# When a hybrid decoder step fetches the gate tiles of its attention projection, and when the rows of the projection after it

## The chip, the cores and the metric

The kernel runs on one core of a Trainium2 chip, as one launch. The metric is the device time of that launch in microseconds (us). Five engines work side by side and meet at semaphores: PE multiplies matrices (PEld is its weight load), DVE and ACT work elementwise, POOL works elementwise and issues accumulating transfers, SP only issues transfers. Each engine takes its instructions in the order in which they stand in its queue; an instruction whose data is late holds all that stand behind it.

## The reference, cut to what matters

One layer of a hybrid decoder on 512 prompt tokens and 8 x 4 sample tokens, 544 columns in all, in float32:

```
u   = x @ w_in                                   # queries, keys, values, gates of both branches
br_m = layernorm(mlstm(u)) * sigmoid(o_m) * silu(z_m)      # (544, 2048)
br_a = sliding_window_attention(u) * silu(z_a)             # (544, 2048)
y    = sigmoid(g_m) * (br_m @ w_proj_m) + sigmoid(g_a) * (br_a @ w_proj_a)
out  = layernorm(alpha * x + y @ w_out)
```

The change lies in `sigmoid(g_a) * (br_a @ w_proj_a)`, called the attention projection below, and at its border with `br_m @ w_proj_m`, the next projection. Both weights are 2048 x 2048. The kernel keeps float32 accuracy on a PE that multiplies a reduced format: each operand is split into a high part (`h`) and a low part (`l`), and a product is high x high + low x high + high x low.

## The kernel before, in words

Everything is stored transposed: an output tile is 128 of the 2048 output columns by 544 tokens, so a projection has 16 output tiles (`ct`). In the attention projection tiles 0 to 7 and 14, 15 are computed one by one (`plain_a`, 96 matmuls each), and tiles 8 to 13 two by two (`paired` over `pair_a`).

A pair computes its two tiles by seven half-size products instead of eight (Winograd's form of Strassen's scheme). The 2 x 2 blocks of the weights are `b11`, `b12`, `b21`, `b22` (128 x 8 x 128 each, 512 KB): two are loaded into buffers of the pool `wr` (tag `raw`, 3 of them), two into `wr2` (tag `raw2`, 3 of them), which also holds a sum, `t1`. `prepare` makes the weight sums, some on DVE (line 679), some by a transfer from POOL that adds in place (line 677, for `b12` += `b22` and `b21` += `b11`), and `split` casts a block to its high part on ACT (line 208, `wh`) and takes the low part on DVE (line 209, `wl`). `half_product` runs 16 matmuls with `wh` (line 699) and 8 with `wl` (line 701). `gather` collects banks into the two outputs `O1`, `O2`. When product 6 is done, `end` multiplies them by the gate tiles `sg` (line 1787, DVE) and stores the result to `d_t` (line 1788, SP). Product p of the first of the three pairs is called P0 to P6 here, and the pairs are the first, second and third.

The gate tiles are the stored `sigmoid(g_a)`, 128 x 544 each (272 KB), fetched by `early` (line 1782) into the pool `c5`, which has two buffers. A third gate tile therefore has to wait until the product of an earlier one has left for `d_t`. `paired` calls `early` at step 2 of a pair, or at the step that the pair names in `early_at`.

The activations of a pair are sums of the rows of `br_a` that were stored earlier (`stored_sums`, read back from `d_sa` by POOL, line 1732, and split on ACT and DVE, lines 257 and 258).

Around the pairs, two more streams of rows are fetched. `branch` (line 1463) loads the sixteen 272 KB rows of `br_m`, `d_brm`, for the next projection and splits them; `operand_sums` (line 1698) loads the same rows two at a time (544 KB) from POOL for the sums of that projection's pairs, two loads ahead.

The order of instructions within each queue is set by a scheduler, which places an instruction by its own timeline; `tc.issue_after(x)` keeps an instruction behind `x`, and `tc.high_priority` lifts it. `state["load"]` is the last weight load so far, `state["cast"]` and `state["split"]` the last weight split. So where the source calls a load need not be where it is issued: a load whose buffer is free can be issued far ahead of its place in the program.

Of the kernel before, what the change touches and what calls it, by code (L numbers as in the profile page):

```python
# [18 lines left out]
ALU = mybir.AluOpType  # L19
# [55 lines left out]
def _build(tc, nc, i, o, es):  # L75
# [12 lines left out]
    V, A, G, PE = nc.vector, nc.scalar, nc.gpsimd, nc.tensor  # L88
# [43 lines left out]
    state = {}  # L132

    def tick():

        with ExitStack() as place:
            if state.get("end"):
                place.enter_context(tc.issue_after(state["end"].ins))
            for g in list(live):
                if next(g, StopIteration) is StopIteration:  # L140
                    live.remove(g)

    def drain():
        while live:
            tick()
# [189 lines left out]
    for g in range(8):  # L335
        for q in range(2):
            k = g * 2 + q
# [321 lines left out]
    def raw2():  # L659
        return wr2.tile([128, 8, 128], F32, tag="raw2", name=nm("raw2"))  # L660

    def load_a(w):
        w["b11"], w["b12"] = (load_half(w["wv"], c0, 0) for c0 in (w["cA"], w["cB"]))

    def load_b(w):
        for n, c0 in (("b22", w["cB"]), ("b21", w["cA"])):
            w[n] = raw2()
            state["load"] = nc.sync.dma_start(w[n][:], w["wv"][:, 8:16, c0:c0 + 128])

    def prepare(w, n):  # L670


        def add(out, a, b):
            if w.get("acc") and out == a and n != 2:
                loaded = state.get(("sums", 13))
                with tc.issue_after(loaded.ins) if loaded else ExitStack():
                    G.dma_start(out=w[out][:], in_=w[b][:], accum_op=ALU.add)  # L677
            else:
                V.tensor_tensor(out=w[out][:], in0=w[a][:], in1=w[b][:], op=ALU.add)  # L679
        if n == 1:  # L680
            w["t1"] = raw2()
            add("t1", "b11", "b12")
        elif n == 2:
            add("b11", "t1", "b22")
        w["hl", n] = split(w[("b11", "t1", "b11", "b21", "b12", "b22", "b21")[n]])
        if n == (1 if w.get("acc") else 3):
            add("b12", "b12", "b22")
        elif n == (3 if w.get("acc") else 4):
            add("b21", "b21", "b11")
# [42 lines left out]
    def paired(work, plain=None, rest=()):  # L732

        steps = [(w, n) for w in work for n in range(7)]
        ready = 0
        with tc.issue_after(state["load"].ins):
            load_a(work[0])
            load_b(work[0])
        for at, (w, n) in enumerate(steps):

            while ready < min(at + 3, len(steps)):
                with tc.high_priority(offset=AHEAD), tc.issue_after(plain.ins) if plain else ExitStack():
                    prepare(*steps[ready])
                ready += 1
            p = at // 7 + 1
            if p < len(work):
                if n == 3:
                    load_a(work[p])
                elif n == 4:
                    load_b(work[p])  # L750
            if n == w.get("early_at", 2) and "early" in w:
# [602 lines left out]
    esF, ahead, PF = ExitStack(), [], KT  # L1354
# [97 lines left out]
    def branch(src, p, tmp, ahead=(), order=(0, 1, 2, 3)):  # L1452
        hs, los = [None] * 4, [None] * 4
        for q in order:
            hs[q], los[q] = (p.tile([128, 4, T], F32R, tag="act", name=nm(n)) for n in ("bh", "bl"))

        def steps():
            for k in range(KT):
                if k < len(ahead):
                    st = ahead[k]  # L1460
                else:
                    st = tmp(k)
                    nc.sync.dma_start(st[:], src[k])
# [205 lines left out]
    wm, wa_, wo = kview("w_proj_m"), kview("w_proj_a"), kview("w_out")  # L1669
# [21 lines left out]
    def operand_sums(src, to, p, far=2, pinned=False):  # L1691

        def behind(name):
            return tc.issue_after(state[name].ins) if pinned else ExitStack()

        def load(k):
            t_ = tx.tile([128, 2, T], F32, tag="tx", name=nm("tx"))
            G.dma_start(out=t_[:], in_=src[k:k + 9:8].rearrange("k p t -> p k t"))
            return t_

        ahead = [load(k) for k in range(far)]
        for k in range(8):
            for _ in range(2):
                yield
            t_ = ahead.pop(0)
            r11, r21, r12, r22 = (t_[:, a, c:c + HT] for a in range(2) for c in (0, HT))
            for name in ("s1", "n2", "n3", "s4"):
                if name not in to:
                    to[name] = quad(p, name)
            with behind("split"), behind("cast"):  # L1710
                four_sums(r11, r12, r21, r22, r22, r12)
                for name, r_ in (("s1", r22), ("n2", r11), ("n3", r21), ("s4", r12)):
                    hilo(r_, to[name][0][:, k], to[name][1][:, k])
            if k + far < 8:
                ahead.append(load(k + far))
# [58 lines left out]
    def pair_a(ct):  # L1774

        sgs = []

        def early():
            for c in (ct, ct + 1):
                sg = c5t()  # L1780
                with tc.issue_after(state["load"].ins):
                    nc.sync.dma_start(sg[:], d_sga[c])
                sgs.append(sg)

        def end(o1, o2):
            for c, sg, o in zip((ct, ct + 1), sgs, (o1, o2)):
                V.tensor_tensor(out=sg[:], in0=o[:], in1=sg[:], op=ALU.mult)
                nc.sync.dma_start(d_t[c], sg[:])
        return dict(wv=wa_, x=XA, cA=ct * 128, cB=ct * 128 + 128, scale=1.0, acc=True, end=end, early=early,
                    early_at=4)  # L1790

    LEAD_A, PAIR_A, TAIL_A = 6, 8, 14
    marks = []
# [39 lines left out]
    state["end"] = None  # L1833
    drain()
    esB2.close()
    tx = pool(esR, "txc", 2)
# [274 lines left out]
    for g in range(G3):  # L2111
        ct = 16 - G3 + g
# [125 lines left out]
```

## Time and profile before

| what | value |
|---|---|
| median of 3 runs | 2449.86 us (2449.78 to 2451.84) |
| the profiled execution | 2449.24 us, of which the span of instructions is 2447.5 us |
| PE busy | 2427.9 us, 99% of the span |
| DVE, ACT, POOL busy | 1910.0, 1252.3 and 532.5 us |
| granted TensorE clock, mean | 0.997 of full speed |
| transfers | 479.88 MB, mean 196 GB/s |
| three pairs of the attention projection | about 1971 to 2042 us of the span |

Times inside the span are counted in us from its start. A row of the timeline gives start, duration, engine, line, operation, output and inputs, and, in brackets, how long the engine had been idle and what released it. Matmuls overlap, so the distance from one start to the next is their pace, not the duration in the row. A row of the table of stretches gives the length of the stretch, the busy time of PE, PEld, DVE, ACT and POOL with the number of instructions, the granted clock, the busy share of the 16 DMA engines and the GB/s moved; the share can read a little over 1.

### The profile page before, as it was taken

The page shows a single profiled execution, that of the slowest core. Times are in us where ns is not written, and L with a number is a line of the kernel's source. Part 1 is how long each engine was busy: PE and PEld are TensorE (multiplying, and loading weights), DVE is VectorE, ACT ScalarE, POOL GpSimd, SP SyncE. Part 2 cuts the span into 40 slices and gives each one's busy share as a digit, 9 for nine tenths or more (in the row PEclk, how much of TensorE's full clock was granted, in tenths as well). Part 3 has the DMA queues.
Part 4 walks back from the last instruction along what each step waited for, and adds up shares of the span by engine and source line. Part 5 has one row for each costly group of instructions (what it writes and reads, how often), then busy time and mean ns, then how long its engine had stood idle before and what let it go on. Part 6 is the DMA issues. An engine that isn't in the chain of part 4 may idle for free.

```text
span 2447.5 us, 49023 instructions
## 1 busy us (share of the span) xinstructions
PE 2427.9 (99%) x19394; PEld 2374.8 (97%) x19394; DVE 1910.0 (78%) x2879; ACT 1252.3 (51%) x2074; POOL 532.5 (22%) x509
## 2 busy tenths in 40 slices
PE   8999999999999999999999999999999999999998
PEld 8999999999999999999999999999999999999997
DVE  7868888888888888987877888878766566877666
ACT  5456676676666665443433444544644444434432
POOL 3114334333333430211111221211000120111111
PEclk9999999999999999999999999999999999999999
DMA  6876666667777655677677586686765488898776
GB/s 178 202 173 158 160 163 148 160 152 177 169 171 177 165 145 144 153 228 241 180 251 242 167 244 208 187 248 213 249 203 168 168 244 244 233 235 271 200 218 204
DMA packets 569597, 479.88 MB, mean 196 GB/s; under 512 B 48664, under 2 KB 464136, under 8 KB 569112
## 3 DMA queue, kind: packets, MB, share of 16 engines
q1 hardware_dynamic: 550776, 411.22, 56.8%
q0 software_dynamic: 18112, 64.76, 13.5%
q8 instruction: 152, 2.49, 0.4%
q10 hardware_dynamic: 480, 0.79, 0.1%
q14 instruction: 77, 0.63, 0.1%
HBM read 326.35 MB, written 100.77 MB: 175 GB/s over the span
## 4 chain that ended last, share of the span: by engine, by line
PE 98%; DVE 1%; issue 0%; ACT 0%; SPq 0%; DMA 0%; DVEq 0%; ACTq 0%
PE bank L699 49%; PE bank L701 24%; PE bank L218 10%; PE sm L1528 2%; PE sm L218 2%; PE bank L1335 1%; PE sm L1567 1%; PE sm L814 1%; PE sm L1583 1%; PE sm L865 1%; PE sm L2047 1%; PE sm L840 1%; PE sm L1340 1%; PE bank L421 0%; PE sm L1515 0%
## 5 line engine op out<-in xcount | busy, mean ns | idle before, releaser
L208 ACT CAST wh<-raw 128x1024 fp32r<-128x1024 f32 x641 | 672.0, 1048 | 826.3 <-PE bank L699 698.3
L209 DVE TENSOR_TENSOR wl<-raw,wh 128x1024 fp32r<-128x1024 f32 x641 | 803.8, 1255 | 196.5 <-ACT wh L208 182.5
L699 PE MATMUL bank<-xk,wh 128*128 128x272 f32 x2336 | 323.4, 289 | 0.0
L679 DVE TENSOR_TENSOR raw<-raw,raw 128x1024 f32<-128x1024 f32 x244 | 309.7, 1270 | 10.1 <-DMA raw<-in_w_in 2.7
L699 PEld LDWEIGHTS bank<-xk,wh 128*128 128x128 f32 x2336 | 303.4, 188 | 1.9 <-issue 1.4
L718 POOL TENSOR_TENSOR ev<-p,ev 128x272 f32<-128x272 f32 x85 | 118.3, 1392 | 461.1 <-ACT ev L717 428.5
L699 PE MATMUL bank<-n2h,wh 128*128 128x272 f32 x656 | 170.0, 291 | 0.0
L701 PE MATMUL bank<-xk,wl 128*128 128x272 f32 x1168 | 169.8, 287 | 0.0
L699 PE MATMUL bank<-n3h,wh 128*128 128x272 f32 x656 | 169.5, 291 | 0.2 <-ACT wh L208 0.2
L699 PE MATMUL bank<-s1h,wh 128*128 128x272 f32 x656 | 169.6, 291 | 0.0
L699 PE MATMUL bank<-n2l,wh 128*128 128x272 f32 x656 | 167.9, 287 | 0.0
L699 PE MATMUL bank<-n3l,wh 128*128 128x272 f32 x656 | 167.7, 288 | 0.0
L699 PE MATMUL bank<-s4h,wh 128*128 128x272 f32 x656 | 167.5, 289 | 0.0
L699 PE MATMUL bank<-s1l,wh 128*128 128x272 f32 x656 | 167.3, 287 | 0.0
L699 PE MATMUL bank<-s4l,wh 128*128 128x272 f32 x656 | 167.0, 287 | 0.0
L701 PEld LDWEIGHTS bank<-xk,wl 128*128 128x128 f32 x1168 | 155.6, 188 | 0.1
L677 POOL DMA_DIRECT2D raw<-raw x96 | 83.2, 867 | 314.2 <-DVE ev L726 217.7
L699 PE MATMUL bank<-a11h,wh 128*128 128x272 f32 x584 | 150.5, 289 | 0.0
L699 PE MATMUL bank<-a11l,wh 128*128 128x272 f32 x584 | 149.4, 288 | 0.0
L699 PEld LDWEIGHTS bank<-n3h,wh 128*128 128x128 f32 x656 | 123.4, 188 | 2.1 <-issue 1.2
L699 PEld LDWEIGHTS bank<-s1h,wh 128*128 128x128 f32 x656 | 123.2, 188 | 1.6 <-issue 1.0
L699 PEld LDWEIGHTS bank<-n2h,wh 128*128 128x128 f32 x656 | 123.4, 188 | 1.2 <-issue 1.2
(552 smaller groups left out, 5805.4 us busy)
## 6 DMA issues: line engine op xcount, KB each, us to landing
raw<-in_w_in SPq DMA_DIRECT2D x296, 512.0 KB
raw<-raw POOLq DMA_DIRECT2D x96, 512.0 KB, 5.0
C<-in_state_mlstm_C SPq DMA_DIRECT2D x32, 1024.0 KB
out<-C SPq DMA_DIRECT2D x64, 512.0 KB
raw<-in_w_proj_a SPq DMA_DIRECT2D x32, 512.0 KB
raw<-in_w_proj_m SPq DMA_DIRECT2D x32, 512.0 KB
raw<-in_w_out SPq DMA_DIRECT2D x32, 512.0 KB
d_v<-ev SPq DMA_DIRECT2D x16, 272.0 KB
```

Of the source, the lines that this page charges most:

```text
L208: state["cast"] = A.copy(wh[:, k:k + n], raw[:, k:k + n])
L209: state["split"] = V.tensor_tensor(out=wl[:, k:k + n], in0=raw[:, k:k + n], in1=r32(wh[:, k:k + n]), op=ALU.subtract)
L218: PE.matmul(ps[f][:, :w], a[:, kk], b(k, c, w), start=(k == 0 and n == 0), stop=(k == 15 and n == 2))
L677: G.dma_start(out=w[out][:], in_=w[b][:], accum_op=ALU.add)
L679: V.tensor_tensor(out=w[out][:], in0=w[a][:], in1=w[b][:], op=ALU.add)
L699: PE.matmul(ps, wh[:, k], x(p, k), start=(first and k == 0 and p == 0), stop=False, skip_group_check=True)
L701: state["end"] = PE.matmul(ps, wl[:, k], x(0, k), start=False, stop=(k == 7), skip_group_check=True)
L718: G.tensor_tensor(out=c22, in0=p1, in1=c11, op=ALU.subtract)
L814: PE.matmul(pp[:, c0 + w0:c0 + 256], qs[a][:, j * 128:j * 128 + 128], kx[:, k0:k0 + 256 - w0], start=(n == 0), stop=(n == 1))
L840: PE.transpose(pt[:, b * 128:b * 128 + 128], s_[:, b, 128:256], ident)
L865: PE.matmul(po[:, b * 128:b * 128 + n], VA[:, b], p_[:, 2 * b:2 * b + n // 128], start=(b == 0 and m == 0), stop=(b == 3 and m == 1), skip ...
L1528: state["cells"] = PE.matmul(pp[:, 0:258], a[:, b * 128:b * 128 + 128], b_[:, b, f], start=(b == 0 and n == 0), stop=(b == 3 and n == 2))
```

## The change

Three edits.

- **Gate tiles.** The pairs of the attention projection no longer name `early_at`; `early` is called at step 2 and not at step 4.
- **Rows on SP.** The loads of `branch` are kept behind `pairs_loaded`, the last weight load of the three pairs, once that name is set, that is, for `d_brm` alone.
- **Rows on POOL.** The first two loads of `operand_sums` for `d_brm` are kept behind `summed`, the last adding transfer of the three pairs.

No instruction is added or removed on any engine.

```
--- before.py
+++ after.py
@@ -674,7 +674,7 @@
             if w.get("acc") and out == a and n != 2:
                 loaded = state.get(("sums", 13))
                 with tc.issue_after(loaded.ins) if loaded else ExitStack():
-                    G.dma_start(out=w[out][:], in_=w[b][:], accum_op=ALU.add)
+                    state["summed"] = G.dma_start(out=w[out][:], in_=w[b][:], accum_op=ALU.add)
             else:
                 V.tensor_tensor(out=w[out][:], in0=w[a][:], in1=w[b][:], op=ALU.add)
         if n == 1:
@@ -748,7 +748,7 @@
                     load_a(work[p])
                 elif n == 4:
                     load_b(work[p])
-            if n == w.get("early_at", 2) and "early" in w:
+            if n == 2 and "early" in w:
                 w["early"]()
             if at == 4:
                 for _ in rest:
@@ -1460,7 +1460,8 @@
                     st = ahead[k]
                 else:
                     st = tmp(k)
-                    nc.sync.dma_start(st[:], src[k])
+                    with tc.issue_after(state["pairs_loaded"].ins) if "pairs_loaded" in state else ExitStack():
+                        nc.sync.dma_start(st[:], src[k])
                 with tc.issue_after(state["cast"].ins), tc.issue_after(state["split"].ins):
                     hilo(st[:], hs[k // 4][:, k % 4], los[k // 4][:, k % 4])
                 yield
@@ -1698,7 +1699,8 @@
             G.dma_start(out=t_[:], in_=src[k:k + 9:8].rearrange("k p t -> p k t"))
             return t_
 
-        ahead = [load(k) for k in range(far)]
+        with tc.issue_after(state["summed"].ins) if pinned else ExitStack():
+            ahead = [load(k) for k in range(far)]
         for k in range(8):
             for _ in range(2):
                 yield
@@ -1786,8 +1788,7 @@
             for c, sg, o in zip((ct, ct + 1), sgs, (o1, o2)):
                 V.tensor_tensor(out=sg[:], in0=o[:], in1=sg[:], op=ALU.mult)
                 nc.sync.dma_start(d_t[c], sg[:])
-        return dict(wv=wa_, x=XA, cA=ct * 128, cB=ct * 128 + 128, scale=1.0, acc=True, end=end, early=early,
-                    early_at=4)
+        return dict(wv=wa_, x=XA, cA=ct * 128, cB=ct * 128 + 128, scale=1.0, acc=True, end=end, early=early)
 
     LEAD_A, PAIR_A, TAIL_A = 6, 8, 14
     marks = []
@@ -1831,6 +1832,7 @@
     XA = operands((bah_, bal_), SA)
     paired([pair_a(ct) for ct in range(PAIR_A, TAIL_A, 2)], state["split"], rest=sums_)
     state["end"] = None
+    state["pairs_loaded"] = state["load"]
     drain()
     esB2.close()
     tx = pool(esR, "txc", 2)
```

The scheduler turns these into the following orders. In the queue of SP, from the last weight load of the first pair on (`raw` is a weight block, `c` a tile of 128 x 544, `d_sga` the gates, `d_brm` the rows for the next projection, `d_t` the stored product), this stood before:

```order
L668 DMA raw_3321_24341<-in_w_proj_a 128x8x128
L1463 DMA c_3416_25122<-d_brm 128x544
L1772 DMA d_t<-c_3308_24204 128x544
L668 DMA raw_3345_24499<-in_w_proj_a 128x8x128
L1463 DMA c_3420_25144<-d_brm 128x544
L195 DMA raw_24466<-in_w_proj_a 128x8x128
L195 DMA raw_24697<-in_w_proj_a 128x8x128
L668 DMA raw_3346_24501<-in_w_proj_a 128x8x128
L1782 DMA c_3347_24503<-d_sga 128x544
L1782 DMA c_3348_24505<-d_sga 128x544
L1788 DMA d_t<-c_3348_24505 128x544
L668 DMA raw_3372_24730<-in_w_proj_a 128x8x128
```

and this stands in the changed kernel:

```order
L668 DMA raw_3321_24341<-in_w_proj_a 128x8x128
L1784 DMA c_3338_24432<-d_sga 128x544
L1774 DMA d_t<-c_3308_24204 128x544
L668 DMA raw_3347_24503<-in_w_proj_a 128x8x128
L1784 DMA c_3339_24434<-d_sga 128x544
L195 DMA raw_24470<-in_w_proj_a 128x8x128
L195 DMA raw_24701<-in_w_proj_a 128x8x128
L668 DMA raw_3348_24505<-in_w_proj_a 128x8x128
L1790 DMA d_t<-c_3339_24434 128x544
L668 DMA raw_3374_24734<-in_w_proj_a 128x8x128
L1790 DMA d_t<-c_3338_24432 128x544
L1784 DMA c_3365_24667<-d_sga 128x544
```

The first pair's two gate tiles stood behind the second pair's weights `raw_24466` and `raw_3346` and the third pair's `raw_24697`. They now stand in the places of the two early rows, one ahead of the store of `c_3308`, one right behind `raw_3347`. The second pair's first gate tile follows the first pair's stores, at the end of the piece.

The next piece of the same queue, before:

```order
L1788 DMA d_t<-c_3347_24503 128x544
L195 DMA raw_24699<-in_w_proj_a 128x8x128
L195 DMA raw_25056<-in_w_proj_a 128x8x128
L668 DMA raw_3373_24732<-in_w_proj_a 128x8x128
L1782 DMA c_3374_24734<-d_sga 128x544
L1782 DMA c_3375_24736<-d_sga 128x544
L1788 DMA d_t<-c_3375_24736 128x544
L1782 DMA c_3397_24957<-d_sga 128x544
L1788 DMA d_t<-c_3374_24734 128x544
L1782 DMA c_3398_24959<-d_sga 128x544
L1463 DMA ev_25074<-d_brm 128x544
```

and in the changed kernel:

```order
L1784 DMA c_3366_24669<-d_sga 128x544
L195 DMA raw_24703<-in_w_proj_a 128x8x128
L195 DMA raw_25056<-in_w_proj_a 128x8x128
L668 DMA raw_3375_24736<-in_w_proj_a 128x8x128
L1464 DMA c_3416_25122<-d_brm 128x544
L1464 DMA c_3420_25144<-d_brm 128x544
L1790 DMA d_t<-c_3366_24669 128x544
L1784 DMA c_3392_24898<-d_sga 128x544
L1790 DMA d_t<-c_3365_24667 128x544
L1784 DMA c_3393_24900<-d_sga 128x544
L1464 DMA ev_25074<-d_brm 128x544
```

The second pair's gate tiles (`c_3374`, `c_3375` before; `c_3365`, `c_3366` now) moved from behind the third pair's last weights, `raw_3373`, to ahead of its `b12`, `raw_24699` (now `raw_24703`). The two early rows, `c_3416` and `c_3420`, now stand behind the last weights, `raw_3375`.

In the queue of POOL, in the first pair, this stood before (`raw<-raw` are the adding transfers, `ev` an elementwise step of `gather`):

```order
L677 DMA raw_3321_24341<-raw_24335 128x1024
L1698 DMA tx_25388<-d_brm 128x2x544
L1698 DMA tx_25390<-d_brm 128x2x544
L677 DMA raw_24466<-raw_3345_24499 128x1024
L718 TENSOR_TENSOR ev_24660<-p_3357_24627,ev_24659 128x272
L677 DMA raw_3346_24501<-raw_24464 128x1024
L677 DMA raw_24699<-raw_3372_24730 128x1024
L718 TENSOR_TENSOR ev_24891<-p_3384_24858,ev_24890 128x272
L677 DMA raw_3373_24732<-raw_24697 128x1024
```

and in the changed kernel:

```order
L677 DMA raw_3321_24341<-raw_24335 128x1024
L677 DMA raw_24470<-raw_3347_24503 128x1024
L718 TENSOR_TENSOR ev_24660<-p_3357_24627,ev_24659 128x272
L677 DMA raw_3348_24505<-raw_24468 128x1024
L677 DMA raw_24703<-raw_3374_24734 128x1024
L718 TENSOR_TENSOR ev_24891<-p_3384_24858,ev_24890 128x272
L677 DMA raw_3375_24736<-raw_24701 128x1024
L1699 DMA tx_25388<-d_brm 128x2x544
L1699 DMA tx_25390<-d_brm 128x2x544
```

The two loads of 544 KB, `tx_25388` and `tx_25390`, stood between the first pair's last adding transfer and the second pair's first one. They now stand behind the third pair's last one.

Two neighbours on ACT change places in the first pair (the cast of the second weight block now stands ahead of that of one row of sums), and the matching two on DVE; on PE, only matmuls' waits follow from that. The order of DVE around line 1787 (1789 in the changed kernel) is unchanged.

More of the change, by code (lines that the diff above doesn't have):

```diff
@@ L676, in add @@
                 with tc.issue_after(loaded.ins) if loaded else ExitStack():
-                    G.dma_start(out=w[out][:], in_=w[b][:], accum_op=ALU.add)
+                    state["summed"] = G.dma_start(out=w[out][:], in_=w[b][:], accum_op=ALU.add)
             else:
@@ L750, in paired @@
                     load_b(work[p])
-            if n == w.get("early_at", 2) and "early" in w:
+            if n == 2 and "early" in w:
                 w["early"]()
@@ L1462, in steps @@
                     st = tmp(k)
-                    nc.sync.dma_start(st[:], src[k])
+                    with tc.issue_after(state["pairs_loaded"].ins) if "pairs_loaded" in state else ExitStack():
+                        nc.sync.dma_start(st[:], src[k])
                 with tc.issue_after(state["cast"].ins), tc.issue_after(state["split"].ins):
@@ L1699, in load @@
             return t_
-        ahead = [load(k) for k in range(far)]
+        with tc.issue_after(state["summed"].ins) if pinned else ExitStack():
+            ahead = [load(k) for k in range(far)]
         for k in range(8):
@@ L1788, in end @@
                 nc.sync.dma_start(d_t[c], sg[:])
-        return dict(wv=wa_, x=XA, cA=ct * 128, cB=ct * 128 + 128, scale=1.0, acc=True, end=end, early=early,
-                    early_at=4)
+        return dict(wv=wa_, x=XA, cA=ct * 128, cB=ct * 128 + 128, scale=1.0, acc=True, end=end, early=early)
     LEAD_A, PAIR_A, TAIL_A = 6, 8, 14
@@ L1833, in _build @@
     state["end"] = None
+    state["pairs_loaded"] = state["load"]
     drain()
```

## The prediction

> **What bounds the kernel now.** I read the chain that ended last first, then the waits of PE over the whole span (group, total us, times, longest).
>
> ```profile
> PE 98%; DVE 1%; issue 0%; ACT 0%; SPq 0%; DMA 0%; DVEq 0%; ACTq 0%
> ...
> PE bank L699 <- ACT wh L208: 4.6, 2, 4.4
> ...
> PE bank L701 <- DVE wl L209: 0.4, 1, 0.4
> ```
>
> PE sets the end, and a microsecond saved elsewhere is worth nothing unless PE waits for it. It waits little: once 4.4 us for a weight cast and once 0.4 for a low part of weights. Both lie in the three pairs, so the table of stretches comes next.
>
> ```profile
> core 0: us, PE busy (x) PEld busy (x) DVE busy (x) ACT busy (x) POOL busy (x), PEclk, DMA share, GB/s
> 1971.00:1989.00 18.00, 18.00 (x146) 17.97 (x145) 14.42 (x21) 11.28 (x19) 7.59 (x7) 1.00 1.02 269
> 1989.00:1999.00 10.00, 8.64 (x67) 8.20 (x66) 3.85 (x4) 2.45 (x3) 0.91 (x1) 1.00 1.12 324
> 1999.00:2008.00 9.00, 5.80 (x28) 5.81 (x29) 5.93 (x7) 3.03 (x5) 0.39 (x1) 0.62 0.45 134
> 2008.00:2026.00 18.00, 17.76 (x142) 17.53 (x141) 10.84 (x13) 6.68 (x8) 2.72 (x3) 1.00 0.80 193
> 2026.00:2042.50 16.50, 16.35 (x130) 16.35 (x131) 10.38 (x14) 8.21 (x12) 2.48 (x2) 1.00 0.63 167
> 2042.50:2062.00 19.50, 19.50 (x159) 19.50 (x158) 12.30 (x18) 10.20 (x16) 0.00 (x0) 1.00 1.02 337
> ```
>
> Up to 1999 the DMA engines are full; then they run dry (0.45) while PE stands, and the granted clock falls to 0.62. How much the pairs lose in all follows from two rows of the chain (start, duration, what):
>
> ```profile
> 1971.25 2.02 PE bank L699 x16
> ...
> 2042.47 57.60 PE bank L218 x461
> ```
>
> The second gives PE's pace, 57.60 / 461 = 0.125 us per matmul. Three pairs of seven products of 24 matmuls are 504, or 63.0 us; they take 2042.47 - 1971.25 = 71.2. So 8.2 us is all that can be won here. PE's timeline shows most of it, in products 1 and 2 of the second pair:
>
> ```profile
> 1995.61 0.29 PE L699 MATMUL bank<-sumh,wh 128*128 128x272 f32 x1
> ...
> 2002.20 0.59 PE L699 MATMUL bank<-sumh,wh 128*128 128x272 f32 x1 [4.41 <-ACT wh L208]
> 2002.59 0.43 PE L699 MATMUL bank<-suml,wh 128*128 128x272 f32 x1
> ...
> 2006.89 0.43 PE L699 MATMUL bank<-sumh,wh 128*128 128x272 f32 x1
> ...
> 2008.55 0.29 PE L699 MATMUL bank<-bh,wh 128*128 128x272 f32 x1
> ```
>
> The two products are 48 matmuls, 6.0 us, and take 2008.55 - 1995.61 = 12.9: **6.9 us lost**. The pause is 2002.20 - (1995.61 + 16 x 0.125) = 4.6; the other 2.3 is pace: from 2002.59 to 2006.89 lie 19 matmuls, 0.226 us each.
>
> Who is late shows on DVE and ACT:
>
> ```profile
> 1992.11 1.22 DVE L679 TENSOR_TENSOR raw<-raw,raw 128x1024 f32<-128x1024 f32 x1
> 1999.13 0.73 DVE L1787 TENSOR_TENSOR c<-ev,c 128x544 f32<-128x544 f32 x1 [5.80 <-issue]
> 1999.77 1.22 DVE L679 TENSOR_TENSOR raw<-raw,raw 128x1024 f32<-128x1024 f32 x1
> ...
> 2001.26 1.22 DVE L209 TENSOR_TENSOR wl<-raw,wh 128x1024 fp32r<-128x1024 f32 x1
> ...
> 1993.44 1.05 ACT L208 CAST wh<-raw 128x1024 fp32r<-128x1024 f32 x1 [3.03 <-DVE raw L679]
> 2001.10 1.04 ACT L208 CAST wh<-raw 128x1024 fp32r<-128x1024 f32 x1 [6.61 <-DVE raw L679]
> ```
>
> DVE stands 5.80 us at line 1787, the product of the first pair with its gate tile. Behind it in DVE's queue are the sum for the second pair's product 2 (1999.77), whose cast at 2001.10 releases PE, and the low part for product 1 (2001.26). The row names no releaser ("issue"), but line 1787 needs only the outputs and the gate tile. The output it takes was finished before 1992.11 (line 726 stands ahead of that row), so the tile is left. SP's rows agree:
>
> ```profile
> 1989.41 4.48 SPq L1782 DMA_DIRECT2D c<-d_sga  x2
> ...
> L1782 SPq DMA_DIRECT2D c<-d_sga x6: 319/382/4002, 1989.4 to 2029.3; - x6
> ```
>
> The first of the two took 4.0 us to issue (the maximum of its line), so the second left at 1989.41 + 4.0 + some 0.1, about 1993.5, behind three weight blocks and two 544 KB loads, and DVE went on at 1999.13, when the DMA engines ran dry.
>
> **The change part by part.** *Gate tiles of the first pair.* The two loads (272 KB each) move from 1989 to the places of the two early rows. The first needs the store of a tile that left ahead of the first pair's weights. The second waits for the store of `c_3308`, and the second pair's `b12` is queued behind it on SP:
>
> ```profile
> 1973.94 0.34 SPq L1772 DMA_DIRECT2D d_t<-c  x1
> ...
> 1983.72 5.00 SPq L195 DMA_DIRECT2D raw<-in_w_proj_a  x2
> ...
> SPq L1782 <- DMA d_t<-c: 4.0, 2, 2.2
> ...
> DMA to landing us min/median/max: 5.6/6.1/8.4
> ```
>
> How fast a store lands in this full stretch isn't shown. From below it is the longest wait of a gate load for such a store, 2.2 us; from above the slowest landing of the adding transfers, 8.4. That is 1976.1 or 1982.3 for the issue, and both lie before 1983.72, when `b12` goes anyway: cost 0. I take 2.2 plus a landing of 6.1: the tile is there at about 1982, at the upper end (twice 8.4) at 1990.7, and DVE wants it at 1993.2. So DVE's 5.80 us go.
>
> *What is late next.* DVE then runs 1992.11 sum, 1993.2 gate product (0.64 to the next row), 1993.9 sum (1.22) to 1995.1. ACT casts to 1996.2; product 2 is due at 1995.61 + 2.0 = 1997.6: 1.4 us to spare. Behind it on DVE stands line 728, which needs product 6:
>
> ```profile
> 1992.74 1.17 PE L701 MATMUL bank<-bh,wl 128*128 128x272 f32 x8
> ```
>
> Its eight matmuls with the low part are through at 1992.74 + 1.0 = 1993.7, so line 728 does not wait. It takes 0.4, and the low part ends at 1995.4 + 1.2 = 1996.6; PE wants it after 12 matmuls of product 2, at 1999.1. Nothing replaces the pause, and with it goes the slow pace: **6.9 us**.
>
> The Trainium skill ("TensorE: Matmul & The Clock Gate", Part 1) says that the array drops to half rate after an idle window of about 3.4 us and returns after about 3.4 us of work. By that estimate the slow pace would cost 1.7 us instead of the 2.3 measured, and the forecast would be 0.6 later; the rows decide. The 0.39 us wait at 2026.15, in a stretch with a clock of 1.00, agrees that a short pause costs only itself.
>
> *Gate tiles of the second pair.* They move ahead of the third pair's `b12`. The second now waits on SP for the store at 2003.14, with `b12` (2010.35) and the last weights behind it:
>
> ```profile
> 2003.14 0.37 SPq L1788 DMA_DIRECT2D d_t<-c  x1
> 2010.35 4.62 SPq L195 DMA_DIRECT2D raw<-in_w_proj_a  x2
> ```
>
> Between them are 7.2 us, which shift together. With a landing of 2.2 the wait is hidden with 5.0 to spare; with 8.4 `b12` goes 1.2 later. Its sum on DVE and what the edit removes:
>
> ```profile
> 2017.01 1.22 DVE L679 TENSOR_TENSOR raw<-raw,raw 128x1024 f32<-128x1024 f32 x1
> ...
> 2022.75 0.73 DVE L1787 TENSOR_TENSOR c<-ev,c 128x544 f32<-128x544 f32 x1 [3.04 <-issue]
> ...
> 2025.47 0.29 PE L699 MATMUL bank<-suml,wh 128*128 128x272 f32 x1
> 2026.15 1.28 PE L701 MATMUL bank<-sumh,wl 128*128 128x272 f32 x8 [0.39 <-DVE wl L209]
> ```
>
> The sum is done at 2018.2 and cast by 2019.3, while product 1 begins at 2025.47 - 15 x 0.125 = 2023.6: 4.3 to spare, so `b12` costs 0 at both ends. Line 1787 blocks DVE once more, for 3.04, and PE loses 2026.15 - 2025.47 - 0.125 = 0.55, and some 0.1 in the first matmul after it, whose row is 1.28 long where the others of eight have 1.16: **0.7 us**.
>
> *Rows on POOL and SP.* Four loads, 2 x 272 and 2 x 544 KB or 1.7 MB, leave the stretch up to 1989 and go behind the third pair's weights, where the shares are 0.80 and 0.63. They save no instruction. At 324 GB/s the two on POOL (1.1 MB) are 3.4 us of full DMA engines, freed while the second pair's weights land. I price that at 0: it shortens transfers that PE does not wait for once the tile is early. From above it is worth the late start of product 6 in the first pair, which needs an adding transfer:
>
> ```profile
> 1988.20 1.16 PE L701 MATMUL bank<-sumh,wl 128*128 128x272 f32 x8
> 1989.50 0.39 PE L699 MATMUL bank<-bh,wh 128*128 128x272 f32 x1
> ```
>
> It begins 1989.50 - (1988.20 + 1.0) = 0.3 late. From below the loads cost what the last rival says; their users come late:
>
> ```profile
> 2056.23 1.05 ACT L208 CAST wh<-raw 128x1024 fp32r<-128x1024 f32 x1
> ...
> 2074.40 0.44 DVE L880 TENSOR_TENSOR tx<-tx 128x272 f32<-128x272 f32 x1
> ```
>
> Line 880 is the first to read the POOL loads, 32 us behind the end of the pairs. The two neighbours that change places on ACT and on DVE make a row of sums later by one cast, 1.05 us; it is used by the fifteenth matmul of product 1, 1.75 us into it. I price that at 0, at worst 0.3.
>
> **Sum.** 6.9 + 0.7 = 7.6 us. From 2042.47 the chain stays on PE without a break for the 57.60 us quoted, and 98% of it is PE, so all of it reaches the end. The profiled execution took 2449.24, so 2441.6; the median of the runs stands 0.6 above it: **2442.3 us**.
>
> **The rivals.** *The early tiles crowd the first pair* (0.18). Its sums and adding transfers run in the stretch with share 1.02, and the gate tiles enter it up to 5 us ahead of the rows they replace. At 269 GB/s the two are 2.1 us. If all of that lands on products 4 to 6, of which the last already begins 0.3 late, the time is 2444.4; for it speaks the full share, against it that as many bytes leave the same stretch. A rule of the Trainium skill ("DMA: Bandwidth & Descriptors", "Queues, rings and completion order") speaks for it: the semaphore of a transfer lands only after all earlier writes of that DMA engine, on any queue, so early loads on SP hold up POOL's. No row read here shows it.
>
> *The tile isn't what DVE waits for, or it is not there earlier* (0.10). The row says "issue", not a transfer. Then the pause stays and the time is 2449.9; against it stands that the same line stops DVE twice.
>
> *The rows come too late for the next projection* (0.06), the slower end. The 1.7 MB are pushed into the stretch from 2042.5, which is full (1.02), and ACT casts rows and weights in one queue. The tightest weights are those cast at 2056.23, ready at 2057.3 and used 18 us (144 matmuls) after 2042.47, at 2060.5: 3.2 to spare. It costs PE from a delay of 3.2 us on, and makes the kernel slower from 3.2 + 7.6 = 10.8 on. At the 167 GB/s of the stretch before, 1.7 MB are 10.2 us; PE would stand 7.0 and lose 2.3 at the slow pace, which is 2442.3 + 9.3 = 2451.6, and more if they land slower. Against it: the stretch they go to has a third of its DMA time free.
>
> **How the numbers follow.** My forecast has 0.66, between 2441.2 (the last 0.6 of the 8.2 won too, and 0.5 of scatter) and 2443.4. The range runs on to 2446.5, past the crowding case with 2 us for a pause that also slows the clock; what it leaves out holds 0.16. About 0.2%, 4.9 us, can be told from no change. Faster by that (below 2445.0): the forecast and 0.12 of the crowding, 0.78. Within it: 0.06 of the crowding and the second rival, 0.16. Slower: 0.06.
>
> **What would show it.** Right: no idle time of DVE ahead of the gate product in either pair; PE's waits of 4.4 and 0.4 gone; a clock of 1.00 from 1989 to 2008; the pairs 63.5 to 64 us long; nothing new from 2035 on. Wrong: a wait of PE for line 699's sums or an adding transfer in the first pair (crowding); line 1789 still waiting 5 us; ACT waiting for `d_brm` with PE behind it.

## The result, and the profile after

The changed kernel takes 2442.73 us (median of 7 runs, 2440.14 to 2444.3) where the kernel before takes 2449.86 (7 runs beside it, 2448.18 to 2451.84): a ratio of 0.9968, with a 95% interval of 0.9956 to 0.9979. It is faster by some 7.1 us, and 2442.3 was predicted. The profiled execution took 2442.73, its span 2440.9.

The waits of PE over the whole span of the changed kernel (group, total us, times, longest), those from 0.5 up:

```profile
PE sm L307 <- DMA cc<-in_consts: 3.2, 1, 3.2
PE sm L340 <- ACT a21h L257: 3.1, 1, 3.1
PE bank L218 <- DVE xk L258: 0.5, 1, 0.5
PE bank L699 <- ACT wh L208: 0.5, 2, 0.3
```

The 4.4 us for a weight cast are gone and so is the 0.4 for a low part. What is left in the pairs is 0.3. The table of stretches, cut where the first four of before were cut or near it:

```profile
core 0: us, PE busy (x) PEld busy (x) DVE busy (x) ACT busy (x) POOL busy (x), PEclk, DMA share, GB/s
1971.00:1989.00 18.00, 18.00 (x145) 17.91 (x144) 14.11 (x21) 11.13 (x20) 6.16 (x5) 1.00 1.02 278
1989.00:1999.00 10.00, 9.70 (x77) 9.48 (x77) 9.04 (x11) 4.99 (x6) 0.86 (x1) 1.00 0.82 195
1999.00:2008.00 9.00, 9.00 (x74) 9.00 (x73) 4.03 (x4) 3.30 (x5) 2.23 (x2) 1.00 0.83 209
2008.00:2020.00 12.00, 12.00 (x98) 12.00 (x97) 9.40 (x11) 5.10 (x6) 0.83 (x1) 1.00 0.90 246
```

From 1999 to 2008 PE did 74 matmuls at a clock of 1.00 where it had done 28 at 0.62, and the DMA engines no longer run dry there (0.83 in place of 0.45). DVE in the first pair, at the place where it stood 5.80 us, and in the second, where it stood 3.04:

```profile
1992.65 1.22 DVE L679 TENSOR_TENSOR raw<-raw,raw 128x1024 f32<-128x1024 f32 x1
1993.78 0.72 DVE L1789 TENSOR_TENSOR c<-ev,c 128x544 f32<-128x544 f32 x1
1994.42 1.22 DVE L679 TENSOR_TENSOR raw<-raw,raw 128x1024 f32<-128x1024 f32 x1
...
2013.78 0.72 DVE L1789 TENSOR_TENSOR c<-ev,c 128x544 f32<-128x544 f32 x1
```

Neither row of line 1789 names any idle time before it: the gate product now runs when its turn comes. The pairs begin and end on PE with these rows:

```profile
1971.36 0.29 PE L699 MATMUL bank<-bh,wh 128*128 128x272 f32 x1
...
1988.58 1.16 PE L701 MATMUL bank<-sumh,wl 128*128 128x272 f32 x8
1990.04 0.39 PE L699 MATMUL bank<-bh,wh 128*128 128x272 f32 x1 [0.30 <-ACT wh L208]
...
2035.25 0.41 PE L218 MATMUL bank<-bh,wh 128*128 128x272 f32 x2
```

They take 2035.25 - 1971.36 = 63.9 us, against 71.2 before and the 63.0 that 504 matmuls take at 0.125 us each. I call what lies above 63.0 the loss of the pairs; it fell from 8.2 to 0.9. More than half of what is left is one place: product 6 of the first pair begins 1990.04 - (1988.58 + 1.0) = 0.46 late, and its first matmul is 0.1 long; before it was 0.3 late, with the same 0.1. Of the 7.3 us won in the pairs 6.6 reach the span: the pairs began 0.3 later (0.2 of it stands already behind the pause at line 340, which ended at 12.64 in place of 12.46), and what follows them took 405.7 where it had taken 405.2.

SP's queue shows that the tiles went where they were sent, and how long a store takes to land, which I had left between two bounds:

```profile
1965.34 3.24 SPq L1784 DMA_DIRECT2D c<-d_sga  x1
1974.18 0.34 SPq L1774 DMA_DIRECT2D d_t<-c  x1
1975.36 0.38 SPq L668 DMA_DIRECT2D raw<-in_w_proj_a  x1
1982.62 0.32 SPq L1784 DMA_DIRECT2D c<-d_sga  x1
1984.50 4.76 SPq L195 DMA_DIRECT2D raw<-in_w_proj_a  x2
```

The second gate tile takes the buffer that the store of 1974.18 empties. It left at 1982.62, that is 8.4 us after that store was issued; 6.8 of them SP stood waiting for the store.

### The profile page after: what moved, and what is told of

The parts are those of the page before. It is cut to its first block, busy times and chain, and to the rows that moved or that the text cites. A ratio compares the mean times of both kernels' runs of the same rounds, so it can differ in the third digit from the quotient of the medians.

```text
span 2440.9 us, 49025 instructions
## 1 busy us (share of the span) xinstructions
PE 2425.6 (99%) x19394; PEld 2372.5 (97%) x19394; DVE 1910.2 (78%) x2879; ACT 1252.0 (51%) x2074; POOL 533.8 (22%) x509
## 4 chain that ended last, share of the span: by engine, by line
PE 97%; DMA 2%; DVE 1%; ACT 0%; issue 0%; SPq 0%; DVEq 0%; POOLq 0%; ACTq 0%
PE bank L699 49%; PE bank L701 24%; PE bank L218 10%; PE sm L1529 2%; PE bank L1335 1%; PE sm L1568 1%; PE sm L814 1%; PE sm L1584 1%; PE sm L865 1%; PE sm L218 1%; PE sm L2049 1%; DMA raw<-raw 1%; PE sm L840 1%; PE sm L1340 1%; DMA raw<-in_w_out 1%; DMA raw<-in_w_proj_a 0%
```

## The experiments

All medians stand beside runs of the kernel before on the same chip: 2450.24 us for the first four, 2449.36 for the next four, 2451.08 for the last three. "Loss" is that of the pairs in the one profiled execution of each kernel, by the same reading as above.

| kernel | median, us | ratio to before, 95% interval | loss, us |
|---|---|---|---|
| before | 2449.86 | | 8.2 |
| changed | 2442.73 | 0.9968 (0.9956 to 0.9979) | 0.9 |
| 1 changed, again | 2442.80 | 0.9968 (0.9956 to 0.9981) | 1.2 |
| 2 gate tiles alone | 2443.81 | 0.9976 (0.9966 to 0.9985) | 3.1 |
| 3 rows alone | 2446.37 | 0.9980 (0.9972 to 0.9989) | 4.4 |
| 4 gate tiles at step 3 | 2441.13 | 0.9961 (0.9947 to 0.9975) | 0.5 |
| 5 without the POOL edit | 2440.91 | 0.9965 (0.9953 to 0.9978) | 0.9 |
| 6 without the SP edit | 2440.71 | 0.9965 (0.9952 to 0.9979) | 0.6 |
| 7 before, gate tiles loaded twice | 2450.72 | 1.0003 (0.9994 to 1.0012) | 9.2 |
| 8 changed, three buffers | 2441.02 | 0.9967 (0.9954 to 0.9979) | 0.3 |
| 9 gate tiles alone, three buffers | 2443.47 | 0.9969 (0.9957 to 0.9980) | 1.5 |
| 10 step 3 and three buffers | 2442.31 | 0.9964 (0.9951 to 0.9978) | 2.0 |
| 11 changed, a third time | 2442.62 | 0.9967 (0.9954 to 0.9979) | 1.1 |

### 1. The changed kernel again

No edit.

> The changed kernel once more, beside the three below. Every theory: 2442.7 us, that is 7 us below the kernel before; no wait of DVE ahead of the gate product.

Measured: 2442.80 us, ratio 0.9968, loss 1.2; product 6 of the first pair 0.4 late, plus 0.1. It repeats the result, and is the measure for the three kernels that ran beside it.

### 2. The gate tiles alone

Against the changed kernel, the rows go back to their early places:

```
-                    with tc.issue_after(state["pairs_loaded"].ins) if "pairs_loaded" in state else ExitStack():
-                        nc.sync.dma_start(st[:], src[k])
+                    nc.sync.dma_start(st[:], src[k])
...
-        with tc.issue_after(state["summed"].ins) if pinned else ExitStack():
-            ahead = [load(k) for k in range(far)]
+        ahead = [load(k) for k in range(far)]
```

> Only the gate tiles move; the four row loads stay early. Theory (the place of the gate tile in SP's queue makes the pause): no idle time of DVE ahead of the gate product in either pair, PE's waits of 4.4 and 0.4 us gone, 2442.3 to 2444, the upper end if the fuller DMA stretch delays product 6 of the first pair by 1 to 2 us. Rival (the 1.7 MB of rows fill the DMA engines, and their leaving makes the gain): the second pair's weights or the tile still land late, PE still loses 4 us or more there, 2447 or more.

Measured: 2443.81 us, loss 3.1. The gate product waits for nothing, as in the changed kernel. But a new wait stands one instruction ahead of it on DVE, and PE stands behind that; this is the timeline of DVE, and below it that of PE:

```profile
1995.48 1.23 DVE L679 TENSOR_TENSOR raw<-raw,raw 128x1024 f32<-128x1024 f32 x1 [3.51 <-DMA raw<-in_w_proj_a]
1996.62 0.72 DVE L1787 TENSOR_TENSOR c<-ev,c 128x544 f32<-128x544 f32 x1
```

```profile
1994.39 1.16 PE L701 MATMUL bank<-bh,wl 128*128 128x272 f32 x8
1997.91 0.40 PE L699 MATMUL bank<-sumh,wh 128*128 128x272 f32 x1 [2.37 <-ACT wh L208]
1998.15 0.29 PE L699 MATMUL bank<-suml,wh 128*128 128x272 f32 x1
1998.28 0.29 PE L699 MATMUL bank<-sumh,wh 128*128 128x272 f32 x1
```

The sum of line 679 is `t1` of the second pair, `b11` + `b12`, and `b12` is the block that SP issues behind the second gate tile. Here are SP's rows of this kernel, and the two of POOL that fall into the same microseconds:

```profile
1984.34 0.32 SPq L1782 DMA_DIRECT2D c<-d_sga  x1
1984.75 1.11 SPq L1463 DMA_DIRECT2D c<-d_brm  x1
1985.96 2.54 SPq L195 DMA_DIRECT2D raw<-in_w_proj_a  x2
```

```profile
1984.94 0.74 POOL L1698 DMA_DIRECT2D tx<-d_brm  x1 [1.72 <-DVE suml L258]
1986.64 0.72 POOL L1698 DMA_DIRECT2D tx<-d_brm  x1 [0.95 <-DVE suml L258]
```

The block left at 1985.96, which is 15.0 us after the pairs began (1970.98 here; 12.6 before, 13.1 in the changed kernel), and flew for 9.5 us beside 1.1 MB of POOL's. So the rows' edits, which I had priced at 0, save some 2 us in the profiled executions once the tile is early (a loss of 3.1 without them against 0.9 to 1.2 with them). The medians put it at 1.0 (2443.81 against 2442.80), and their intervals overlap: the named wait shows the effect, and its size is known only roughly. A pause of 2.37 us left the pace at 0.125 us per matmul from the second matmul on: no slow pace follows it.

### 3. The rows alone

Against the changed kernel, the gate tiles go back to step 4:

```
-            if n == 2 and "early" in w:
+            if n == w.get("early_at", 2) and "early" in w:
...
-        return dict(wv=wa_, x=XA, cA=ct * 128, cB=ct * 128 + 128, scale=1.0, acc=True, end=end, early=early)
+        return dict(wv=wa_, x=XA, cA=ct * 128, cB=ct * 128 + 128, scale=1.0, acc=True, end=end, early=early,
+                    early_at=4)
```

> Only the rows move; the gate tiles stay behind the weights on SP. Theory (place in the queue): the tile still goes out at about 1989.8 at the earliest, lands 6.1 us later at 1995.9 against 1993.2 wanted, with 1.4 us to spare on the way to PE: a pause of about 1.3 us without a slow stretch, and the second pair's 0.7 us stays; 2444.3 (2443.3 to 2446). Rival (rows): all of the first pair's pause goes, 2442.5 to 2443.4.

Measured: 2446.37 us, loss 4.4. That is above the range of the theory (2443.3 to 2446), and the pause is 2.5 us where 1.3 was worked out. SP, DVE and PE of this kernel:

```profile
1989.86 2.15 SPq L1784 DMA_DIRECT2D c<-d_sga  x2
```

```profile
1997.66 0.73 DVE L1789 TENSOR_TENSOR c<-ev,c 128x544 f32<-128x544 f32 x1 [3.87 <-DMA c<-d_sga]
```

```profile
2000.73 0.39 PE L699 MATMUL bank<-sumh,wh 128*128 128x272 f32 x1 [2.48 <-ACT wh L208]
```

The wait now bears its name: the gate tile's transfer. It was "issue" in the profile of before, at the same line, in the same place of the same queue. With 1.7 MB gone from the stretch the two issues take 2.15 us in place of 4.48, the tile is there 1.6 us sooner after the start of the pairs, and DVE and PE each wait 1.93 us less (3.87 for 5.80, 2.48 for 4.41). Products 1 and 2 lose 2.8 in place of 6.9, since the slow pace of 2.3 us is gone as well: a pause of 2.48 did not bring it, one of 4.41 did. The whole loss falls by 3.8; the rest went into small gaps, the largest 0.29 at 1979.58. The small pause of the second pair stays (0.45 us at 2022.51).

### 4. The gate tiles between the two weight loads

Against the changed kernel, `early` is called at step 3:

```
-            if n == 2 and "early" in w:
+            if n == w.get("early_at", 2) and "early" in w:
...
-        return dict(wv=wa_, x=XA, cA=ct * 128, cB=ct * 128 + 128, scale=1.0, acc=True, end=end, early=early)
+        return dict(wv=wa_, x=XA, cA=ct * 128, cB=ct * 128 + 128, scale=1.0, acc=True, end=end, early=early,
+                    early_at=3)
```

> As changed, but the gate tiles asked for at step 3: they stand on SP right behind the second pair's b12 and ahead of the third pair's b11, not in the first pair's full stretch. Theory: landed by 1991 to 1994, no pause worth more than 0.5 us; the late start of product 6 (0.56 us in the changed kernel) falls back to 0.3 to 0.4, 2442 to 2443.5. Crowding as the cause of that late start: 2442.3; if the tile is too late here: a DVE wait of 1 to 3 us ahead of the gate product and 2444 to 2446.

Measured: 2441.13 us (2440.3 to 2441.68), loss 0.5. SP:

```profile
1982.09 0.37 SPq L195 DMA_DIRECT2D raw<-in_w_proj_a  x1
1982.51 2.21 SPq L1784 DMA_DIRECT2D c<-d_sga  x2
1986.77 0.38 SPq L195 DMA_DIRECT2D raw<-in_w_proj_a  x1
```

The tiles stand behind the second pair's `b12`, the one block that must not be late, and ahead of the third pair's `b11`, which has time. They are there for the gate product (no idle time ahead of it), and no store's landing stands in front of `b12`. Product 6 of the first pair begins 0.2 late, plus 0.1. The time lies 0.9 below the range expected. It is the lowest ratio here, but its interval holds that of the changed kernel's median.

### 5 and 6. Which rows hold `b12` back

In experiment 5 the POOL edit is taken out of the changed kernel, in experiment 6 the SP edit; each is one half of the diff of experiment 2.

> The changed kernel without its edit on POOL: the gate tiles are early and the two rows on SP (0.55 MB) go late, but the two 544 KB loads on POOL (1.1 MB) leave early again. Theory (the rows are worth 2 to 2.5 us because they take bytes out of the stretch in which the second pair's b12 lands, and the POOL loads are two thirds of the bytes): PE stands some 1.5 to 2.5 us before product 2 of the second pair, DVE waits for raw weights and not for the gate tile, pairs lose 2.5 to 3, time 2443.4 to 2443.9. Rival (it is SP's two rows that hold up b12, because they stand ahead of it in SP's own queue): nothing is lost against the changed kernel, pairs lose about 1.2, time 2442.4 to 2442.9.

> The changed kernel without its edit on SP: the gate tiles are early and POOL's two loads go late, but the two rows of 272 KB on SP leave early again, ahead of the gate tiles or b12. Theory (POOL's bytes decide): pairs lose 1.1 to 1.8, PE's pause before product 2 is below 1 us, time 2442.4 to 2443.2. Rival (SP's own queue decides): b12 is issued 1.5 us or more later than the 1984.50 of the changed kernel, PE stands about 2.5 us, pairs lose about 3, time 2443.8.

Measured: 2440.91 us and loss 0.9; 2440.71 us and loss 0.6. Both times are 1.5 us or more below the lowest that was expected. Neither brings the pause back, so the theory that POOL's bytes decide fell with experiment 5, and its rival, SP's queue, with experiment 6. Rows of SP and DVE, first without the POOL edit, then without the SP edit:

```profile
1982.42 5.01 SPq L195 DMA_DIRECT2D raw<-in_w_proj_a  x2
...
1990.81 1.22 DVE L679 TENSOR_TENSOR raw<-raw,raw 128x1024 f32<-128x1024 f32 x1
```

```profile
1985.21 2.55 SPq L195 DMA_DIRECT2D raw<-in_w_proj_a  x2
...
1991.15 1.22 DVE L679 TENSOR_TENSOR raw<-raw,raw 128x1024 f32<-128x1024 f32 x1
```

The pairs began at 1969.52 and 1970.12. In 5 the block left 12.9 us into the pairs, flew beside POOL's loads and was there at 21.3, when DVE had its turn for the sum: at most 8.4 us. In 6 it left at 15.1, as late as in experiment 2, but without POOL's loads beside it, and was there at 21.0: at most 5.9. In experiment 2 it had both, 15.0 and 9.5, and was 3.5 late. So it takes both a late start (2.1 us, from the second tile's wait for the store and the row behind it) and a long flight (9.5 us with POOL's loads, at most 5.9 without); DVE is free for the sum only some 21 us into the pairs, and that hides either one. Each of these readings is of a single profiled execution.

### 7. The suspected wait made longer

Against the kernel before:

```
                 with tc.issue_after(state["load"].ins):
                     nc.sync.dma_start(sg[:], d_sga[c])
+                    nc.sync.dma_start(sg[:], d_sga[c])
```

> The kernel before with each gate tile loaded twice in a row into the same buffer, so that the suspected wait has twice the bytes (two more loads of 272 KB in each pair) at the same place of SP's queue. Theory (DVE stands for the gate tile and PE's pause comes from that): DVE's wait before the first pair's gate product grows from 5.8 to about 8 to 10 us, PE's pause from 4.6 to 7 to 9, with a slow pace behind it of about 2.3 us as before (it follows from a pause of enough length, not from its size), the second pair's small pause grows from 0.5 to about 3; time 2454 to 2458. Rival (DVE stands for something else and the tile is there in time): 2449 to 2451.

Measured: 2450.72 us, ratio 1.0003, loss 9.2. The time is that of the rival, but the rows contradict it; DVE, then PE:

```profile
1993.14 1.22 DVE L209 TENSOR_TENSOR wl<-raw,wh 128x1024 fp32r<-128x1024 f32 x1
2000.45 1.46 DVE L1788 TENSOR_TENSOR c<-ev,c 128x544 f32<-128x544 f32 x2 [6.10 <-DMA c<-d_sga]
```

```profile
2003.66 2.18 PE L701 MATMUL bank<-sumh,wl 128*128 128x272 f32 x8 [4.60 <-DVE wl L209]
```

The tile came 3.1 us later in the pairs (2000.45 - 1969.32 = 31.1 against 1999.13 - 1971.09 = 28.0, counted from PE's first row of line 699), and DVE waited for it by name. But the scheduler, which knew of the longer load, had put the sum, line 728 and a low part ahead of the gate product, so PE got through the high part of product 2 before it stood. It stood as long as before (4.60), one step further on. The experiment did not hold DVE's order fixed, and so it is no measure of the slope; that the tile stops DVE and DVE stops PE it shows once more.

### 8. A third buffer for the gate tiles

Against the changed kernel:

```
-    c5 = pool(esC, "c5", 2)
+    c5 = pool(esC, "c5", 3)
```

> The changed kernel with three buffers for the gate tiles in place of two, so that the second gate tile of a pair waits for no store to land. In the changed kernel that wait held SP for 8.4 us and b12 left at 1984.50. Theory (the store's wait is hidden, and b12's place is set by the split that frees its buffer): b12 leaves within 0.5 us of 1984.5, the second gate tile leaves about 1968 to 1970, pairs lose 0.8 to 1.5, time within 0.6 of the changed kernel, 2442.2 to 2443.4. Rival (the late second tile in the middle of the full stretch is what makes product 6 late and the adding transfers slow): product 6 begins 0.3 late or less, pairs lose about 0.5, time 2441 to 2441.8, as with the gate tiles behind b12.

Measured: 2441.02 us, loss 0.3. SP:

```profile
1963.98 3.88 SPq L1784 DMA_DIRECT2D c<-d_sga  x2
1972.85 0.32 SPq L1774 DMA_DIRECT2D d_t<-c  x1
1974.02 0.38 SPq L668 DMA_DIRECT2D raw<-in_w_proj_a  x1
1983.15 4.12 SPq L195 DMA_DIRECT2D raw<-in_w_proj_a  x2
```

Both tiles go ahead of the store, and `b12` still leaves 13.16 us into the pairs (1983.15 - 1969.99), as in the changed kernel, 13.14. So the 8.4 us for the store were hidden there: that half of the theory holds, but the time is 1.2 below its range, and the loss below its 0.8. The rival is right in its part: product 6 is not late here at all, the loss is below its 0.5, and the time lies in its range. The time stays within the interval of the changed kernel.

### 9. The gate tiles alone, with the third buffer

The diffs of experiments 2 and 8 together.

> The gate tiles early and all rows early too (as in the second experiment, which lost 3.1 us in the pairs), but with three buffers for the gate tiles, so that neither the second gate tile nor b12 behind it stands in SP's queue for the landing of a store. The bytes in the stretch are the same as there. Theory of two parts (b12 of the second pair came late because it left 2 us later, at 15.0 us after the start of the pairs instead of 12.9, and also flew beside POOL's 1.1 MB; one of the two alone is hidden): b12 leaves at 12.6 to 13.4 us after the start of the pairs, its sum waits under 0.8 us, the pairs lose 0.6 to 1.5, time 2440.5 to 2443. Rival (the sum of bytes decides, wherever b12 stands): the sum waits 2.5 us or more, PE stands about 2, pairs lose 2.5 to 3.5, time 2442.5 to 2444.5.

Measured: 2443.47 us, loss 1.5. SP and DVE; the pairs begin at 1969.67:

```profile
1983.30 5.02 SPq L195 DMA_DIRECT2D raw<-in_w_proj_a  x2
...
1991.70 1.22 DVE L679 TENSOR_TENSOR raw<-raw,raw 128x1024 f32<-128x1024 f32 x1
```

The block left at 13.6 with all the bytes of experiment 2 in flight, and its sum did not wait. That is the theory of two parts, and against the sum of bytes. The 1.5 lie elsewhere, in the first pair: 0.8 where product 6 begins and the rest in four small gaps at 1974.9 to 1979.4. But the median is 0.5 above the upper end expected and lies in the range of the rival, while the profiled execution took 2442.22: for the rows the theory holds, and the median does not bear it out.

### 10 and 11. The two best together, beside the changed kernel

The diffs of experiments 4 and 8 together, and the changed kernel a third time.

> The two best places together: gate tiles right behind the second pair's b12, rows late, and three buffers. Of the 63.0 us that the pairs cannot go below, the two kernels it is made of lost 0.45 and 0.24, so there is nothing to add up: pairs lose 0.2 to 0.6, time 2440.2 to 2441.7, within the scatter of either; against the changed kernel 0.6 to 1 us shorter in the pairs.

> The changed kernel once more on the chip of the two kernels beside it. Pairs lose 0.9 to 1.2 us, product 6 of the first pair begins 0.4 to 0.6 late. At the first pause of the program (line 340, some 12.5 us from the start), two cases by how long PE stands: at 2.7 us or more the granted clock is near 0.63 from 13.5 to 18 and the pairs begin at about 1971.2; at 2.6 or less it is 1.00 there and they begin at about 1969.7. Time 2441 to 2443 by which of the two it falls into.

Measured: 2442.31 us and loss 2.0; 2442.62 us and loss 1.1, with product 6 of the first pair 0.8 late (0.4 to 0.6 was expected). The first is a miss. Some 1.5 us of its loss lie in front of everything that was changed, in the products that use the first pair's own weights; DVE, then PE:

```profile
1974.17 1.23 DVE L679 TENSOR_TENSOR raw<-raw,raw 128x1024 f32<-128x1024 f32 x1 [3.65 <-DMA raw<-in_w_proj_a]
```

```profile
1977.85 1.27 PE L701 MATMUL bank<-sumh,wl 128*128 128x272 f32 x8 [0.74 <-DVE wl L209]
```

DVE waited for these weights in every kernel here, 1.9 to 2.9 us in the others, and here the wait was 3.65. They were issued at the same place of the queue (7.5 us ahead of the pairs); why they landed later in this execution the trace does not say. A single execution can thus lose a microsecond that no edit here explains, and the variants 4, 5, 6, 8 and 10 cannot be told from the changed kernel, nor from each other.

## Why the prediction came out right, step by step

- **Term 1, 6.9 us for the late tile: right.** The pause and the slow pace are gone, clock 1.00 throughout. Experiment 3 settles the second rival's doubt ("issue"): the wait is for `d_sga`. It also shows that the slow pace goes as soon as the pause is shorter: with 1.93 us less of pause all of the 2.3 of slow pace was gone. By the Trainium skill ("TensorE: Matmul & The Clock Gate", Part 1) the slow pace follows an idle window of about 3.4 us; the pauses of 2.37 and 2.48 without it and of 4.41 with it agree. The pauses at the start of the program, in the last section, do not.
- **Term 2, 0.7 us in the second pair: right.** The row of 2013.78 has no idle time before it, and PE has no gap there; experiment 3, which keeps the tiles late, keeps it (0.45).
- **"Cost 0" for the wait behind the store: right, with the wrong value taken.** I took 2.2 us for the landing and it was 8.4, the upper bound; over the kernels here it ran from 8.0 to 10.6. That it cost nothing was forecast for both bounds, and for the reason that held: `b12` was to go no earlier anyway (experiment 8).
- **Rows on POOL and SP, priced at 0: wrong as a step.** "It shortens transfers that PE does not wait for once the tile is early" overlooked that the early tile pushes the row and `b12` back on SP. Without the two edits PE waits for just that transfer, 2.37 us in the profiled execution of experiment 2; either edit is enough to avoid it (5 and 6). The sum was not hurt because I counted the gate tiles at their full 7.6, which they bring only with at least one row edit. In this term the right sum was luck: the change held both kinds of edit. Against the kernel before, whose median beside them was 2450.24, the gate tiles alone won 6.4 us (experiment 2), the rows alone 3.9 (experiment 3) and both 7.4 (experiment 1): the rows shorten the same wait that the gate tiles remove, so the two do not add up.
- **What is late next: right for the changed kernel.** DVE's order of rows came as worked out, sum, gate product, sum, at 1992.65, 1993.78 and 1994.42. The cast for product 2 ended at 1996.8 and product 2 was due at 1996.15 + 2.0 = 1998.15: 1.3 to spare, where 1.4 was forecast. What the forecast asked of `b12` was only when it leaves, not when it lands; experiment 2 shows that its landing is what comes next.
- **Crowding, the first rival: there, but small.** Product 6 of the first pair is 0.4 to 0.8 late in the three executions of the changed kernel against 0.3, where the rival asked for some 2. In the execution shown, the first adding transfer took 9.33 us, above the 8.4 that was the slowest before.
- **Rows too late for the next projection: did not happen.** After the pairs DVE waits 0.5 us for `tx<-d_brm` at line 880 (0.9 before), and PE has no wait behind the pairs that it did not have (in experiment 1 one more, of 0.2 us).
- **The sum.** 7.6 were forecast, 7.3 won in the pairs, 6.5 in the profiled execution (2449.24 to 2442.73) and 7.1 in the medians. The signs named for "right" are all there: no idle time ahead of the gate products, the waits of 4.4 and 0.4 gone, a clock of 1.00 from 1989 to 2008, pairs of 63.9 us.

## What to carry to other kernels

A small load that stands behind big ones in an issue queue can stop an engine for longer than its own size suggests, and the price is paid twice when the pause is long enough to slow the matmul clock (here 4.41 us was, 2.48 was not). Price edits that go together as a set: two edits can work on the same wait, so that their gains do not add up (6.4 and 3.9 us alone, 7.4 together), and one of them can be what keeps a new wait from opening behind the other. And when a wait moves, look one instruction further ahead in the same queue, since that is where the next late transfer shows.

## What the runs showed of the hardware that was not expected

**Near the start of the program, pauses of 2.7 us and more were followed by a slower clock, and pauses of 2.6 and less were not.** At line 340, some 12.5 us in, PE stands for the second time (the first is at the very start, for 3.2 to 3.5 us). Here is that wait on PE in the kernel before and in experiment 8, each with its next stretch:

```profile
12.46 0.63 PE L340 MATMUL sm<-cc,xr 128*128 128x128 f32 x4 [2.72 <-ACT r L349]
...
13.50:18.00 4.50, 4.50 (x27) 4.50 (x26) 3.18 (x9) 3.63 (x12) 4.50 (x4) 0.62 1.10 347
```

```profile
12.82 0.63 PE L340 MATMUL sm<-cc,xr 128*128 128x128 f32 x4 [2.62 <-DMA xr<-in_x_prompt]
...
13.50:18.00 4.50, 4.50 (x40) 4.50 (x39) 3.48 (x10) 3.88 (x13) 4.50 (x4) 1.00 1.11 348
```

After 2.72 us of idle time the clock is 0.62 and PE does 27 matmuls in 4.5 us; after 2.62 it is 1.00 and PE does 40. All 13 profiled executions fall on one side or the other: 2.72, 3.04, 3.11, 3.18 and 3.25 are slow, 1.63 to 2.62 (eight of them) are not. The 13 matmuls are 1.6 us, and the pairs begin at 1971.3 on the mean of the slow ones and at 1969.7 on that of the others. The slow pauses of 2.72 to 3.25 us lie below the 3.4 us that the Trainium skill gives ("TensorE: Matmul & The Clock Gate", Part 1). The pauses in the pairs (2.37 and 2.48 without, 4.41 with) fit both. That the length alone decides is not shown: the slow pauses also begin earlier, at 9.5 to 9.9 us, where the others begin at 10.0 to 10.9. This is a part of the scatter between runs of one kernel (the changed kernel fell once on the slow side and twice on the other), and it lies far ahead of the change; the profiled executions of before and after both had it.

**A store in a full stretch lands late.** 272 KB took 8.0 to 10.6 us from SP's issue until the gate load that needs its buffer went, at a busy share of the DMA engines of 0.92 to 1.06 from 1973 to 1983. In the kernel before, near the end of the pairs, it was 2.3 and 2.6 us (2023.51 to 2025.77 and 2026.76 to 2029.31), at a share of 0.47.
